# Four groups of projections in a two-layer decoder trunk: two matmuls per weight tile in place of three

## The chip, the cores and the metric

One core of one Trainium2 chip runs the whole kernel in one launch. The metric is the device time of one execution in microseconds; the kernel before was run three times, and its median is what a changed kernel is compared with.

## The reference, cut to what matters

The input `x` is 256 tokens by 1024 channels. Each of two layers does three things in turn: a SwiGLU feed-forward net, a mixing block, a second feed-forward net. Everything is float32.

```python
h = h + 0.5 * swiglu(rms_norm(h, ln_ffn1[l]), ffn1_w13[l], ffn1_w2[l])
u = rms_norm(h, ln_mix[l])
z, xbc, dt_raw, cq, ckv, kr, gates = split_cols(u @ w_in[l], IN_SPLIT_SIZES)
y_ssd = ssd_branch(z, xbc, dt_raw, ...)        # conv, Mamba-2 scan, norm, w_ssd_out
y_mla = mla_branch(cq, ckv, kr, ...)           # low-rank queries and keys, attention, w_mla_out
g = jax.nn.sigmoid(gates)
merged = g[..., :D_MODEL] * y_ssd + g[..., D_MODEL:] * y_mla
h = h + merged @ w_o[l]
```

The change touches the columns of `u @ w_in` that give the latents `cq` (512 columns) and `ckv` (256), the rotary key `kr` with `dt_raw` (96 columns, padded to 128), the first 128 channels of both gates, and the product of the attention output with `w_mla_out`.

## The kernel before

Activations lie transposed, 128 channels on the partitions by 256 tokens, and every product is a sum over blocks of 128 input channels. To keep float32 accuracy each operand is split in two parts: a high part in the type fp32r (what a copy to that type leaves) and a low part, the rest. For a weight block the high part `wh` is a cast by ScalarE (L152) and the low part `wl` a subtraction by VectorE (L153); both are at most 128 by 1024 and come from a ring of four buffers filled by a 512 KB load on the SP queue (`ahead`, L144). For an activation, `operand` (L198) makes the two parts and lays them side by side in one tile `[128, blocks, 512]`: 256 columns high, 256 columns low.

A product keeps three of the four partial products. `mm` (L164) makes three matmuls of 256 columns per weight tile, all into the same 256 columns of PSUM: `wh` by the high part (L169), `wh` by the low part (L170), `wl` by the high part (L171). `mm2` (L173) makes two: `wh` by all 512 columns (L178), which leaves two halves side by side in one PSUM bank, and `wl` by the high part into the first half (L179). The two halves must then be added: `halves` (L181) copies the second to SBUF on ScalarE (L182) and adds the first on VectorE (L183). Before the change, `mm2` serves the feed-forward nets, the gates 1 to 7 and the output product of the scan (`wso`); `mm` serves the rest.

The mixing block `mix` (L418) goes in this order. It sums the squares of the residual per token on TensorE and takes an inverse square root in some eight small VectorE instructions (`row_factor`, L245; the last of them, L224, is kept as `self.last`). Inside `issue_after(self.last)` (L437), a block whose VectorE instructions may not be queued ahead of that last one, it runs the products of the un-normalised input `X0` (an `oT` tile) with the blocks `dk` (rotary key and dt), `gate` (two blocks into the two halves of one PSUM bank) and the first of six latents. `latent(i)` (L428) runs one product, then makes an operand of the result for blocks 16 to 21 of tile `A` (ScalarE L204, VectorE L205) and squares it into a sum (`square_into`, L227). ScalarE copies of the gate (L446) and of `dk` (L448) follow. Then the normalised input `X` is built (L449 to L457), between the latents 1 to 3, then latents 4 and 5, then a long chain of small VectorE instructions for `dt` (L501 to L530) that ends in a copy `acum`, its transpose, and a store and reload through DRAM on the POOL queue (`rows`, L537; `row`, L623), on which the decay factors of the scan wait on ScalarE (L648). The loop (L546) begins with the first queries (L695, which read blocks 16 to 19 of `A`), keys and values (`keyval`, L719, blocks 20 and 21) and convolutions (L589).

At the end of `mix`, for each of eight output blocks (L553), two `wso` weight blocks go through `mm2` and `halves`, one `wmo` block goes through `mm`, and VectorE multiplies its PSUM by the second gate (L565), adds the scan's part (L566) and makes an operand of `M`, which the eight `wo` products (L570) read.

There are eight PSUM banks: four for the tag `g` of all these products, two for `s`, two for `h`. The order of the instructions on each engine is not the order of the code: a planner simulates the program with its own costs and issues, on each engine, what is ready, earlier code first. Each engine then runs its queue strictly in that order.

Of the kernel before, what the change touches and what calls it, by code (L numbers as in the profile page):

```python
# [16 lines left out]
ALU = mybir.AluOpType  # L17

P = 128
L = 2  # L20
T = 256
D = 1024
KD = D // P
# [37 lines left out]
class Build:  # L61
# [356 lines left out]
    def mix(self, l, X0, Xn, gain, gain_next):  # L418
        nc, v = self.nc, self.vec[l]
        tt, ts, stt = nc.vector.tensor_tensor, nc.vector.tensor_scalar, nc.vector.scalar_tensor_tensor  # L420
# [4 lines left out]
        A = self.new_A()  # L425
        acc2 = [self.tmp("Rb", [P, T], bufs=1), self.tmp("accs", [P, 2, T], bufs=1)[:, 0, :]]

        def latent(i):  # L428
            q = int(i > 3)
            ps = self.gps()[:, :T]  # L430
            self.mm(ps, self.w("lat"), KD, X0, 0, True, True)
            o = V_QL + i
            self.operand(A, 16 + i, ps, v[:, o:o + 1])
            self.square_into(acc2[q], ps, i in (0, 4))


        with self.tc.issue_after(self.last):  # L437
            ps = self.gps()[:, :T]
            self.mm(ps, self.w("dk"), KD, X0, 0, True, True)
            pg = self.gps()  # L440
            for g in range(2):
                self.mm(pg[:, g * T:(g + 1) * T], self.w("gate"), KD, X0, 0, g == 0, g == 1)
            latent(0)
        Rb = self.bcast(Rt, None)
        gg = self.tmp("g0", [P, 2, T], bufs=1)
        nc.scalar.copy(gg, pg.rearrange("p (g t) -> p g t", g=2))  # L446
        dk = self.tmp("ta", [P, T])
        nc.scalar.copy(dk, ps)  # L448
        X = self.new_X()  # L449
        for n in range(0, KD, 2):  # L450
            u = self.tmp("t2", [P, 2, T])
            for i in range(2):
                stt(out=u[:, i, :], in0=self.hT[:, n + i, :], scalar=gain[:, n + i:n + i + 1], in1=Rb,
                    op0=ALU.mult, op1=ALU.mult)
            hi, lo = X[:, n:n + 2, :T], X[:, n:n + 2, T:]
            nc.scalar.copy(hi, u)
            tt(out=lo, in0=u, in1=hi.bitcast(F32), op=ALU.subtract)  # L457
            if n < 6:
                latent(1 + n // 2)
# [6 lines left out]
        for c in range(2):  # L466
            act(out=tm[:, c, :], in_=pt[:, c * P:(c + 1) * P], func=AF.Copy, scale=Rt[:, c:c + 1])
        latent(4)
        latent(5)

# [3 lines left out]
        ps = self.sps()  # L474
# [36 lines left out]
        q = self.tmp("dtq", [P, 2, 32], bufs=1)  # L511
# [29 lines left out]
        oT = self.new_oT()  # L541
# [11 lines left out]
        for n in range(KD):  # L553
            gg = S["gate", n]
            stt(out=gg[:, 0, :], in0=gg[:, 0, :], scalar=1.0, in1=Rsb, op0=ALU.add, op1=ALU.mult)
            ts(out=gg[:, 1, :], in0=gg[:, 1, :], scalar1=0.5, scalar2=0.5, op0=ALU.mult, op1=ALU.add)
            ps = self.gps()
            self.mm2(ps, self.w("wso"), 8, A, 0, True, False)
            self.mm2(ps, self.w("wso"), 8, A, 8, False, True)
            m = self.tmp("ta", [P, T])  # L560
            self.halves(m, ps)
            tt(out=gg[:, 0, :], in0=gg[:, 0, :], in1=m, op=ALU.mult)
            ps = self.gps()[:, :T]
            self.mm(ps, self.w("wmo"), 8, oT, 0, True, True)
            tt(out=m, in0=gg[:, 1, :], in1=ps, op=ALU.mult)  # L565
            tt(out=m, in0=m, in1=gg[:, 0, :], op=ALU.add)  # L566
            self.operand(M, n, m)
        for n in range(KD):
            ps = self.gps()[:, :T]
# [340 lines left out]
```

## Time and profile before

| | us |
|---|---|
| median of three runs | 1467.56 |
| lowest and highest | 1466.51, 1470.18 |
| the profiled execution | 1469.72 |
| its span, first to last instruction | 1467.8 |
| TensorE busy (matmuls) | 1451.8 |
| VectorE busy | 1114.6 |
| ScalarE busy | 911.8 |

The profiled execution took 2.2 us longer than the median and 1.9 us longer than its own span. A matmul's busy time in the profile overlaps that of the next one, since they are pipelined; how fast a stream of them goes is read from the distance of their starts. "PE" is TensorE, "PEld" its weight loads, "DVE" VectorE, "ACT" ScalarE, "POOL" GpSimd. "L178" is line 178 of the kernel. Tile names are those of the program: `g` a PSUM bank of the products, `wh` and `wl` the weight parts, `oT`, `X` and `A` operand tiles.

### The profile page before, as it was taken

What the parts mean: (1) busy time and instruction counts of PE and PEld (TensorE: products, weight loads), DVE (VectorE), ACT (ScalarE), POOL (GpSimd) and SP (SyncE); (2) the same over time, 40 slices, a digit from 0 to 9 for tenths busy, and PEclk for the clock granted to TensorE, in tenths of its full rate; (3) what the DMA queues carried; (4) which work ended last, traced back from release to release, by engine and by line L of the source; (5) the groups of instructions that cost most, each with busy time, mean ns of one, the idle gap of its engine ahead of it and who ended that gap; (6) DMA issues with size and microseconds to landing.
All of it is one profiled execution on the core that took longest, in us unless ns stands there. A gap on an engine that the chain in (4) does not pass through costs nothing.

```text
span 1467.8 us, 25011 instructions
## 1 busy us (share of the span) xinstructions
PE 1451.8 (99%) x9418; PEld 1304.8 (89%) x9418; DVE 1114.6 (76%) x2080; ACT 911.8 (62%) x1738; POOL 18.5 (1%) x38
## 2 busy tenths in 40 slices
PE   7999999999999999999999999999999999999999
PEld 6888899899888999888888888997998889988888
DVE  7877679888877677777678776888888576688764
ACT  6555556988775456555455554678888654565542
POOL 0000000000000000000000000000000000000000
PEclk9999999999999999999999999999999999999999
DMA  7556655555444555556655566565554445555563
GB/s 254 184 186 178 192 176 182 183 160 157 152 144 158 188 179 188 191 189 183 193 191 191 188 180 195 178 192 155 166 169 139 154 165 190 175 190 193 187 197 109
DMA packets 75977, 261.43 MB, mean 178 GB/s; under 512 B 8880, under 2 KB 11184, under 8 KB 75856
## 3 DMA queue, kind: packets, MB, share of 16 engines
q1 hardware_dynamic: 73232, 251.37, 53.3%
q0 software_dynamic: 2624, 8.46, 1.9%
q8 instruction: 74, 1.21, 0.3%
q14 instruction: 47, 0.39, 0.1%
HBM read 258.68 MB, written 1.11 MB: 177 GB/s over the span
## 4 chain that ended last, share of the span: by engine, by line
PE 97%; DVE 1%; ACT 1%; issue 0%; DMA 0%; SPq 0%; DVEq 0%; ACTq 0%
PE g L178 40%; PE g L179 21%; PE g L169 9%; PE g L170 9%; PE g L171 9%; PE g L695 2%; PE s L658 2%; PE g L719 1%; PE h L780 1%; PE h L779 1%; PE h L761 0%; PE s L635 0%; PE h L803 0%; DVE wl L153 0%; DVE cy L594 0%; PE h L799 0%
## 5 line engine op out<-in xcount | busy, mean ns | idle before, releaser
L152 ACT CAST wh<-st 128x1024 fp32r<-128x1024 f32 (+2 forms) x488 | 500.6, 1027 | 483.5 <-PE g L178 314.7
L153 DVE TENSOR_TENSOR wl<-st,wh 128x1024 fp32r<-128x1024 f32 (+2 forms) x488 | 581.0, 1192 | 258.6 <-ACT wh L152 254.7
L178 PE MATMUL g<-X,wh 128*128 128x512 f32 x928 | 330.8, 399 | 8.0 <-DVE X L205 7.5
L178 PE MATMUL g<-A,wh 128*128 128x512 f32 x938 | 327.6, 395 | 0.0
L179 PE MATMUL g<-X,wl 128*128 128x256 f32 x928 | 262.6, 283 | 0.0
L179 PE MATMUL g<-A,wl 128*128 128x256 f32 x938 | 260.8, 279 | 0.0
L178 PE MATMUL g<-oT,wh 128*128 128x512 f32 x704 | 244.5, 392 | 0.0
L169 PE MATMUL g<-X,wh 128*128 128x256 f32 x768 | 219.6, 287 | 1.2 <-DVE cy L594 1.2
L178 PEld LDWEIGHTS g<-X,wh 128*128 128x128 f32 x928 | 175.8, 189 | 49.3 <-DVE X L205 8.3
L170 PE MATMUL g<-X,wh 128*128 128x256 f32 x768 | 218.7, 285 | 0.0
L171 PE MATMUL g<-X,wl 128*128 128x256 f32 x768 | 218.4, 285 | 0.0
L178 PEld LDWEIGHTS g<-A,wh 128*128 128x128 f32 x938 | 175.7, 188 | 40.1
L179 PE MATMUL g<-oT,wl 128*128 128x256 f32 x704 | 196.9, 280 | 0.0
L179 PEld LDWEIGHTS g<-X,wl 128*128 128x128 f32 x928 | 177.1, 191 | 0.4 <-issue 0.2
L179 PEld LDWEIGHTS g<-A,wl 128*128 128x128 f32 x938 | 176.6, 188 | 0.4
L178 PEld LDWEIGHTS g<-oT,wh 128*128 128x128 f32 x704 | 131.6, 187 | 28.6
L169 PEld LDWEIGHTS g<-X,wh 128*128 128x128 f32 x768 | 146.7, 191 | 3.2 <-issue 1.6
L170 PEld LDWEIGHTS g<-X,wh 128*128 128x128 f32 x768 | 146.9, 191 | 0.7 <-issue 0.5
L171 PEld LDWEIGHTS g<-X,wl 128*128 128x128 f32 x768 | 146.9, 191 | 0.3 <-issue 0.3
L179 PEld LDWEIGHTS g<-oT,wl 128*128 128x128 f32 x704 | 133.0, 189 | 0.2
L170 PE MATMUL g<-oT,wh 128*128 128x256 f32 x272 | 76.8, 283 | 0.0
L171 PE MATMUL g<-oT,wl 128*128 128x256 f32 x272 | 76.6, 284 | 0.0
(286 smaller groups left out, 1831.0 us busy)
## 6 DMA issues: line engine op xcount, KB each, us to landing
st<-in_w_dram SPq DMA_DIRECT2D x238, 512.0 KB, 4.3
st<-in_win_dram SPq DMA_DIRECT2D x124, 512.0 KB, 4.0
st<-in_wso_dram SPq DMA_DIRECT2D x32, 512.0 KB, 4.1
st<-in_w_dram SPq DMA_DIRECT2D x32, 384.0 KB, 3.2
row<-rows POOLq DMA_DIRECT2D x32, 256.0 KB, 3.9
st<-in_wmo_dram SPq DMA_DIRECT2D x16, 512.0 KB, 4.2
st<-in_wo_dram SPq DMA_DIRECT2D x16, 512.0 KB, 3.5
st<-in_wuq_dram SPq DMA_DIRECT2D x16, 384.0 KB, 3.3
```

The source lines that it names most:

```text
L152: self.nc.scalar.copy(wh, st)
L153: self.nc.vector.tensor_tensor(out=wl, in0=st, in1=wh.bitcast(F32), op=ALU.subtract)
L169: mm(out, lhsT=wh[:, k, :], rhs=xh, start=start and k == 0, stop=False)
L170: mm(out, lhsT=wh[:, k, :], rhs=xl, start=False, stop=False)
L171: mm(out, lhsT=wl[:, k, :], rhs=xh, start=False, stop=stop and k == nk - 1)
L178: mm(out, lhsT=wh[:, k, :], rhs=X[:, x0 + k, :], start=start and k == 0, stop=False)
L179: mm(out[:, :T], lhsT=wl[:, k, :], rhs=X[:, x0 + k, :T], start=False, stop=stop and k == nk - 1)
L658: nc.tensor.matmul(py[64 * i:64 * i + 64, q * T + c * P:(q + 1) * T], lhsT=xdt[:, c, f:f + 64], rhs=r[:, i, o:o + n], start=q == 0 and c = ...
L695: nc.tensor.matmul(pc[c], lhsT=aa, rhs=ww, start=k == 0 and i == 0, stop=k == 3 and i == 2)
L719: nc.tensor.matmul(pc[c], lhsT=aa, rhs=ww[:, k, :], start=k == 0 and i == 0, stop=k == 1 and i == 2)
L779: mm(o, lhsT=qkT[:, 0, cs], rhs=qkT[:, 1, ks], start=c == 0, stop=False)
L780: mm(o, lhsT=peT[:, 0, cs], rhs=peT[:, 1, ks], start=False, stop=False)
```

## The change

The three uses below go from `mm` to `mm2` and `halves`. The latent now goes through an SBUF tile of the tag `cy` before its operand and its square; the `dk` result and both gate results go through `halves` inside the block behind `self.last`, where one ScalarE copy each stood after it; the two gate blocks take a PSUM bank each where they shared one. In the output loop the attention product is added up into `m`, and the gate multiplies `m` where it multiplied PSUM.

```diff
         def latent(i):
             q = int(i > 3)
-            ps = self.gps()[:, :T]
-            self.mm(ps, self.w("lat"), KD, X0, 0, True, True)
+            ps = self.gps()
+            self.mm2(ps, self.w("lat"), KD, X0, 0, True, True)
+            lat = self.tmp("cy", [P, 2, T])[:, 0, :]
+            self.halves(lat, ps)
             o = V_QL + i
-            self.operand(A, 16 + i, ps, v[:, o:o + 1])
-            self.square_into(acc2[q], ps, i in (0, 4))
+            self.operand(A, 16 + i, lat, v[:, o:o + 1])
+            self.square_into(acc2[q], lat, i in (0, 4))
 
 
         with self.tc.issue_after(self.last):
-            ps = self.gps()[:, :T]
-            self.mm(ps, self.w("dk"), KD, X0, 0, True, True)
-            pg = self.gps()
+            ps = self.gps()
+            self.mm2(ps, self.w("dk"), KD, X0, 0, True, True)
+            dk = self.tmp("ta", [P, T])
+            self.halves(dk, ps)
+            gg = self.tmp("g0", [P, 2, T], bufs=1)
             for g in range(2):
-                self.mm(pg[:, g * T:(g + 1) * T], self.w("gate"), KD, X0, 0, g == 0, g == 1)
+                ps = self.gps()
+                self.mm2(ps, self.w("gate"), KD, X0, 0, True, True)
+                self.halves(gg[:, g, :], ps)
             latent(0)
         Rb = self.bcast(Rt, None)
-        gg = self.tmp("g0", [P, 2, T], bufs=1)
-        nc.scalar.copy(gg, pg.rearrange("p (g t) -> p g t", g=2))
-        dk = self.tmp("ta", [P, T])
-        nc.scalar.copy(dk, ps)
         X = self.new_X()
...
             tt(out=gg[:, 0, :], in0=gg[:, 0, :], in1=m, op=ALU.mult)
-            ps = self.gps()[:, :T]
-            self.mm(ps, self.w("wmo"), 8, oT, 0, True, True)
-            tt(out=m, in0=gg[:, 1, :], in1=ps, op=ALU.mult)
+            ps = self.gps()
+            self.mm2(ps, self.w("wmo"), 8, oT, 0, True, True)
+            self.halves(m, ps)
+            tt(out=m, in0=gg[:, 1, :], in1=m, op=ALU.mult)
             tt(out=m, in0=m, in1=gg[:, 0, :], op=ALU.add)
             self.operand(M, n, m)
```

## Rows read from the trace of the kernel before

**Rows 1.** The page, busy time (us), share of the span and instructions of each engine.

```profile
PE 1451.8 (99%) x9418; PEld 1304.8 (89%) x9418; DVE 1114.6 (76%) x2080; ACT 911.8 (62%) x1738; POOL 18.5 (1%) x38
```

**Rows 2.** The page, the chain that ended last, shares of the span by engine.

```profile
PE 97%; DVE 1%; ACT 1%; issue 0%; DMA 0%; SPq 0%; DVEq 0%; ACTq 0%
```

**Rows 3.** Busy us (instructions) of PE, PEld, DVE, ACT, POOL by stretch; PEclk, DMA.

```profile
206.00:228.00 22.00, 22.00 (x180) 22.00 (x179) 21.96 (x48) 16.12 (x33) 0.00 (x0) 1.00 0.59 188
228.00:258.00 30.00, 30.00 (x238) 29.40 (x237) 26.82 (x81) 19.20 (x46) 1.71 (x3) 1.00 0.57 183
258.00:288.00 30.00, 27.80 (x193) 23.99 (x193) 26.68 (x57) 30.00 (x73) 3.22 (x6) 0.96 0.62 201
...
470.00:560.00 90.00, 90.00 (x636) 84.25 (x636) 62.29 (x102) 42.84 (x63) 0.00 (x0) 1.00 0.55 181
```

**Rows 4.** Timeline of PE where it waits, in brackets the idle us and what ended it.

```profile
285.73 0.76 PE L719 MATMUL g<-wh,A 128*128 128x512 f32 x1 [2.19 <-DVE sm L794]
...
286.72 1.05 PE L719 MATMUL g<-wh,A 128*128 128x512 f32 x2
287.57 0.63 PE L719 MATMUL g<-wl,A 128*128 128x512 f32 x1
...
1010.01 0.47 PE L719 MATMUL g<-wh,A 128*128 128x512 f32 x1 [1.13 <-DVE cy L594]
...
1013.23 0.39 PE L169 MATMUL g<-X,wh 128*128 128x256 f32 x1 [0.94 <-DVE cy L594]
```

**Rows 5.** Groups of instructions by line and shape: xcount | busy us, mean ns | idle.

```profile
L169 PE MATMUL g<-oT,wh 128*128 128x256 f32 x272 | 76.4, 283 | 0.0
...
L183 DVE TENSOR_TENSOR t<-t,g 128x256 f32<-128x256 f32 x180 | 74.0, 413 | 0.0
L182 ACT COPY t<-g 128x256 f32<-128x256 f32 x180 | 64.6, 361 | 0.5 <-PE g L179 0.5
```

**Rows 6.** Timeline of PE in the output loop: start us, us, instruction, count.

```profile
478.79 0.28 PE L169 MATMUL g<-oT,wh 128*128 128x256 f32 x1
...
481.67 0.40 PE L178 MATMUL g<-A,wh 128*128 128x512 f32 x1
...
487.31 0.28 PE L169 MATMUL g<-oT,wh 128*128 128x256 f32 x1
```

**Rows 7.** Timeline of PE in the second feed-forward net.

```profile
599.83 0.39 PE L178 MATMUL g<-oT,wh 128*128 128x512 f32 x1
...
602.60 0.39 PE L178 MATMUL g<-oT,wh 128*128 128x512 f32 x1
```

**Rows 8.** Timeline of DVE from the mixing block's start, layer 0, then layer 1.

```profile
206.11 3.49 DVE L153 TENSOR_TENSOR wl<-st,wh 128x1024 fp32r<-128x1024 f32 x3
...
226.66 0.42 DVE L234 TENSOR_TENSOR Rb<-Rb,sq 128x256 f32<-128x256 f32 x1
227.00 1.22 DVE L153 TENSOR_TENSOR wl<-st,wh 128x1024 fp32r<-128x1024 f32 x1
...
228.27 0.48 DVE L205 SCALAR_TENSOR_TENSOR A<-g,vec,A 128x256 fp32r<-128x256 f32 x1
...
953.15 0.47 DVE L205 SCALAR_TENSOR_TENSOR A<-g,vec,A 128x256 fp32r<-128x256 f32 x1
```

**Rows 9.** Timelines of DVE and PE, last block of M and its first reader.

```profile
536.07 0.42 DVE L202 TENSOR_TENSOR X<-ta,X 128x256 fp32r<-128x256 f32 x1 [0.47 <-ACT X L201]
...
538.59 0.52 PE L169 MATMUL g<-X,wh 128*128 128x256 f32 x3
```

**Rows 10.** Timeline of PE, first keys and values, layer 0, then layer 1.

```profile
229.84 0.48 PE L719 MATMUL g<-wh,A 128*128 128x512 f32 x1
...
231.09 0.62 PE L719 MATMUL g<-wh,A 128*128 128x512 f32 x2
...
956.28 0.62 PE L719 MATMUL g<-wh,A 128*128 128x512 f32 x2
```

**Rows 11.** Timeline of ACT, first decay factors of layer 0.

```profile
257.76 1.49 ACT L648 ACTIVATE dec<-row,acum 128x256 f32<-128x256 f32 x4 [3.58 <-DMA row<-rows]
```

## The prediction

> **What bounds the kernel.** I read the busy times first, then the chain that ended last, then starts on TensorE's timeline, and last the stretches around the change. TensorE is busy 99% of the span [rows 1], and the chain of waits runs 97% through it [rows 2], so a shorter product pays one for one wherever nothing else holds TensorE up. Both shares say nothing of a single stage, though. Three stretches count here. In the output loop VectorE is busy 62.3 of 90 us and ScalarE 42.8 [rows 3], so there is room. At the start of mix, from 206 to 228 us, VectorE is busy 21.96 of 22 us [rows 3]: there it is full, though TensorE does not yet wait. From 258 to 288 us ScalarE is busy all 30 us and VectorE 26.7, and TensorE loses time: L719 waits 2.19 us in layer 0, and in layer 1 there are waits of 1.13 and 0.94 us [rows 3, 4]. The change adds work to VectorE exactly where it is full.
>
> **What TensorE saves.** The edits touch 8 blocks of 128 channels for dk, 16 for the gates, 48 for six latents and 64 for eight wmo products, 136 in a layer and 272 in all, the count of L169 on `oT` tiles [rows 5]. Each goes from three matmuls of 256 columns to one of 512 and one of 256. The columns are 768 both ways, so only the loss per instruction can shrink. What it is comes from distances of starts:
> - three by 256: a wmo product starts at 478.79 and the next wso product at 481.67, 2.88 us for 8 blocks, 0.360 us a block [rows 6];
> - two: the 16 blocks of wso from 481.67 to 487.31 take 5.64 us, 0.3525 a block [rows 6]; in the second feed-forward net, whose moving operand is the same tag `oT`, eight pairs take 602.60 - 599.83 = 2.77 us, 0.346 a block [rows 7].
>
> So a block gains 0.0075 us (slow pairs) to 0.0135 us (fast pairs). For the 144 blocks at the start of mix I take the fast pair, which has their operand and follows the same kind of stage: 1.9 us. For the 128 blocks of wmo I take the slow pair, measured next to them in the same loop: 1.0 us. Sum 2.9 us; ends 272 x 0.0075 = 2.0 and 272 x 0.0135 = 3.7 us. That is 0.2% of the time.
>
> A page speaks against this. The Trainium skill, page "TensorE: Matmul & The Clock Gate", section "Back-to-back issue gap", puts a matmul of N columns at N/2.4 + 2.5 ns, so that a fused pair saves one floor of 2.5 ns a block; by it 272 blocks would give 0.7 us in place of 2.9, an estimate. By that rule three matmuls of 256 columns would take 3 x 109 = 328 ns, where the trace has 360 [rows 6], so it agrees in the sign and not in the size.
>
> **What VectorE and ScalarE get.** Each product gains one 256-column addition on VectorE and mostly one copy on ScalarE. A lone addition takes 413 ns and a copy 361 ns [rows 5], but a queue that is full goes by distances of starts: an addition of this shape starts at 226.66 and the next instruction at 227.00, 0.34 us [rows 8]. A layer gets nine additions at the start of mix (dk, two gates, six latents) and eight in the output loop.
> - Output loop: 8 x 0.34 = 2.7 us on VectorE and at most 8 x 0.36 = 2.9 us on ScalarE, beside 90 us of TensorE with 27.7 and 47.2 us to spare [rows 3]: nothing. Without that cover it would be 5.4 us on VectorE in both layers. At its end the chain of the last block grows by a copy and an addition, 0.77 us: its low part is written by 536.07 + 0.42 = 536.49 and the first matmul that needs it starts at 538.59 [rows 9], so 2.1 us of cover, less 0.5 us by which TensorE comes earlier. Nothing, unless a weight split of 1.22 us also slips in between; then 0.4 us.
> - Start of mix: 9 x 0.34 = 3.1 us in a full queue. The copies are covered, since ScalarE has 5.9 of 22 us free [rows 3], and the gate and dk copies replace copies. All nine additions are behind `self.last` or later; the splits just behind it run back to back from 206.11 [rows 8], so the idle time ahead of it cannot be used.
> - Banks: before, dk, both gates and the first latent need three of the four `g` banks, after, all four, and the second latent waits until dk's addition, queued right behind the first split, at about 206.11 + 1.16 + 0.34 = 207.6 us. The second latent starts some 2.9 us after the first at the earliest, past 209 us. Nothing; if the planner put all the splits ahead of it, TensorE would wait about 1 us a layer.
> - The operand and the square now read SBUF in place of PSUM. An addition with one input in PSUM takes 413 ns [rows 5], one wholly in SBUF 0.42 us [rows 8]; at 0.01 us for 12 VectorE instructions this is 0.1 us in the full queue, and I take nothing.
>
> **What is late next.** Queued behind the additions on VectorE are the weight splits, the operands and the small chain of dt. The first product to feel it is keyval. The low part of block 21 is done at 228.27 + 0.48 = 228.75 us and read by the matmul at 231.09, 2.34 us of margin; in layer 1 at 953.62 against 956.28, 2.66 us [rows 8, 10]. The backlog of 3.1 us and TensorE's own 0.97 us (72 blocks x 0.0135) turn this into waits of 1.7 and 1.4 us, 3.1 us together, if the planner leaves keyval where it is. If it sees the lateness and moves convolutions ahead, it costs nothing. Both are open; I take half, 1.5 us.
>
> **The sum.** The profiled execution took 1469.72 us: minus 2.9, plus 1.5, gives 1468.3. It stands 2.16 us above the median of the runs, 1467.56, and the same difference on that gives **1466.2 us**. The ends of this case: all lateness and the slow pairs, -2.0 + 3.1 = +1.1, or 1468.7; none and the fast pairs, -3.7, or 1463.9. A measurement of this kernel can tell about 0.3% from no change, 4.4 us, so 1463.2 and 1472.0 are the bounds.
>
> **The rivals.**
> - Slower: the backlog passes on. The decay factors on ScalarE begin when `row` has landed, after 3.58 us idle [rows 11], and the load hangs on the dt chain, which sits in the same VectorE queue. If the 3.2 us that VectorE has free from 228 to 258 us [rows 3] are waits for weight buffers that TensorE frees, they don't take up the backlog; `row` comes up to 3.1 us later in each layer, ScalarE's full stretch starts as much later, and the wait at 285.73 grows. TensorE's gain ahead of it is then worth nothing; 2 x 3.1 - 1.0 (wmo) = +5.2. A longer wait in layer 1 can also bring what layer 0 shows: the granted clock falls (mean 0.96 in that stretch, the level of 1.2 GHz in it) and L719 then runs at (287.57 - 286.72)/2 = 0.43 us a matmul in place of (231.09 - 229.84)/5 = 0.25 [rows 3, 4, 10], 6 x 0.18 = 1.1 us. Together +6.3, 1473.9 us. It decides from the point where `row` is more than about 2.7 us late per layer, for 2 x 2.7 - 1.0 = 4.4. For it: a full VectorE and a full ScalarE. Against: by 228 us TensorE already binds, and a later VectorE then eats its own idle time.
> - Faster by more than 0.3%: the planner's new order happens to spread the work of 258 to 288 us, and the three waits (2.19 + 1.13 + 0.94 = 4.3) and the slow matmuls (1.1) go: -2.9 - 5.4 = -8.3, 1459.3 us. For it: these waits are a matter of order, since layer 0 and layer 1 run the same code and differ. Against: nothing in the edit takes work off either engine in that stretch.
> - The pairs save nothing in their new place: in the output loop the 512-column matmul already takes some 0.3525 - 0.120 = 0.23 us, nearly two of 0.120 [rows 6]. With 0 saved and 0 to 3.1 us of lateness: 1467.6 to 1470.7. Against: both stages measured have pairs faster than 0.360 us [rows 6, 7]. By the section of the Trainium skill named above this would be nearly the case, with 0.7 us saved, an estimate.
>
> **How the numbers follow.** The forecast case gets 0.42, no gain 0.13, the slower one 0.25 and the faster one 0.20. Of the slower case 0.02 and of the faster one 0.03 stay within 0.3%, so: same 0.42 + 0.13 + 0.02 + 0.03 = 0.60, faster 0.17, slower 0.23. The range runs from the forecast's lower end 1463.9 on into the faster case and from 1470.7 into the slower one, to 1461.0 and 1473.0, leaving out about half of each, 2 in 10. The likeliest case alone is 1463.9 to 1468.7.
>
> **What would show it.** Right: L178 on `oT` up by 272 and the lines of `mm` on it gone; starts 0.346 to 0.3525 us apart for a pair in wmo and latents; VectorE still full from 206 to about 231 us; L719 first waiting on VectorE in the order of 1.5 us, or convolutions ahead of it; VectorE's busy time up by 34 x 0.41 = 14 us and ScalarE's by about 10. The slower rival shows `row` landing over 2.7 us later in its layer and waits at the second L719 that have grown. The faster one shows those waits gone. I am wrong in the sum if pairs in wmo start 0.36 us apart, and wrong in the place if TensorE waits in the output loop.

## The result, and the profile after the change

The change made the kernel slower: median 1480.86 us of four runs (1479.45 to 1484.15) against 1467.71 us of the kernel before beside it, a ratio of 1.0093 [1.0079, 1.0107], or 13.1 us. I had forecast 1466.2 us, a range up to 1473.0 and a chance of 0.23 for slower. The execution profiled after the change took 1479.45 us, its span is 1477.6 us; before, the span was 1467.8 us, so the two traces differ by 9.8 us. In all the runs told of below, one execution (of the kernel with the work alone in six buffers) took 4540.4 us, and its ratio leaves it out. New lines shift the numbers: after, the first queries are L698 (before L695), keyval is L722 (L719), the scan's product L661 (L658), the decay factors L651 (L648).

First the page's busy times of the kernel after:

```profile
PE 1452.7 (98%) x9146; PEld 1291.0 (87%) x9146; DVE 1127.6 (76%) x2114; ACT 917.5 (62%) x1768; POOL 18.5 (1%) x38
```

Against [rows 1], VectorE has 13.0 us more (I had 14) and ScalarE 5.7 us more (I had about 10). TensorE is as busy as before, 1452.7 against 1451.8 us, though it has 272 matmuls fewer, and idle for longer. To see where, I cut the kernel at a line that both have: L241 begins a sum of squares on TensorE, once at the end of each stage. From TensorE's timeline of the kernel after (start, length in us):

```profile
203.11 0.50 PE L241 MATMUL s<-ones,acc 128*128 128x1 f32 x4
...
567.24 0.50 PE L241 MATMUL s<-ones,acc 128*128 128x1 f32 x4
...
935.74 0.50 PE L241 MATMUL s<-ones,acc 128*128 128x1 f32 x4
...
1295.20 0.50 PE L241 MATMUL s<-ones,acc 128*128 128x1 f32 x4
```

and of the kernel before:

```profile
203.92 0.51 PE L241 MATMUL s<-ones,acc 128*128 128x1 f32 x4
...
561.49 0.50 PE L241 MATMUL s<-ones,acc 128*128 128x1 f32 x4
...
929.12 0.50 PE L241 MATMUL s<-ones,acc 128*128 128x1 f32 x4
...
1285.44 0.50 PE L241 MATMUL s<-ones,acc 128*128 128x1 f32 x4
```

The mixing block of layer 0 grew from 357.57 to 364.13 us (+6.56), that of layer 1 from 356.32 to 359.46 (+3.14). The mark is not quite the start of the block: TensorE runs products of `dk` and the gates ahead of it, and after the change it runs more of them there. The first of these in layer 1 starts, after the change, at

```profile
929.61 0.40 PE L178 MATMUL g<-oT,wh 128*128 128x512 f32 x1
```

and in the kernel before at

```profile
923.85 0.28 PE L169 MATMUL g<-oT,wh 128*128 128x256 f32 x1
```

That is 6.13 and 5.27 us ahead of the mark; in layer 0 it starts at 196.87 and 198.65, 6.24 and 5.27 us ahead. Counted from these starts the blocks grew by 7.53 and 4.00 us, the nets between them take 362.37 us against 362.36, and the end changed by +0.04; only the first feed-forward net differs otherwise, by -1.78 (the last section tells why it can). The whole loss is in the two mixing blocks. Now the stretches of the two blocks, and those of [rows 3], after (columns as there: length, then busy time of PE, PEld, DVE, ACT, POOL, granted clock, DMA share, GB/s):

```profile
203.11:567.24 364.13, 355.68 (x2433) 318.83 (x2432) 289.04 (x606) 253.48 (x537) 9.22 (x17) 1.00 0.51 164
935.74:1295.20 359.46, 354.56 (x2434) 319.55 (x2432) 287.05 (x597) 252.96 (x536) 9.11 (x17) 1.00 0.51 166
...
206.00:228.00 22.00, 19.74 (x111) 16.49 (x109) 22.00 (x49) 15.14 (x32) 0.00 (x0) 1.00 0.63 196
470.00:560.00 90.00, 90.00 (x579) 81.98 (x578) 67.48 (x120) 45.93 (x72) 0.00 (x0) 1.00 0.56 184
...
385.00:395.00 10.00, 7.39 (x29) 5.20 (x29) 9.77 (x26) 6.41 (x22) 0.00 (x0) 0.83 0.48 159
```

The same blocks in the kernel before:

```profile
203.92:561.49 357.57, 355.38 (x2561) 326.75 (x2560) 281.96 (x589) 250.75 (x522) 9.22 (x17) 1.00 0.52 167
929.12:1285.44 356.32, 353.97 (x2560) 325.33 (x2559) 281.16 (x580) 249.80 (x521) 9.11 (x17) 1.00 0.52 168
```

The time in which TensorE is not busy is the difference of the first two numbers: after 8.45 and 4.90 us, before 2.19 and 2.35. That is 8.8 us of the 11.5; in the rest TensorE shows as busy, though the pairs should have shortened that. What TensorE waited for in the two blocks after (total us, times, longest; layer 0, then layer 1):

```profile
PE h L806 <- ACT pT L804: 3.6, 2, 2.2
PE g L698 <- DVE cy L183: 1.7, 1, 1.7
PE g L722 <- DVE cy L597: 1.4, 1, 1.4
...
PE g L698 <- DVE cy L183: 1.6, 1, 1.6
PE g L169 <- ACT vv L748: 0.9, 1, 0.9
PE s L638 <- DVE rqy L224: 0.8, 1, 0.8
```

Before, layer 0 had one such wait worth a row, the 2.2 us of L719 that I had listed [rows 4]. Now there are two kinds. One stands where the change was made: the first queries wait for a latent's addition (`cy`, L183). The others stand further on, in attention and convolutions: in layer 0 at 287.56 and 290.33 us, near where L719 waited before, and at 388.41, 160 us behind the queries. On TensorE's timeline of the kernel after:

```profile
227.96 0.41 PE L698 MATMUL g<-wh,A 128*128 128x384 f32 x1 [1.75 <-DVE cy L183]
...
232.17 0.47 PE L722 MATMUL g<-wh,A 128*128 128x512 f32 x1 [0.29 <-DVE cy L183]
...
388.41 0.70 PE L806 MATMUL h<-pT,vv 128*128 128x256 f32 x2 [2.20 <-ACT pT L804]
...
390.26 1.05 PE L722 MATMUL g<-wh,A 128*128 128x512 f32 x2
391.12 0.63 PE L722 MATMUL g<-wl,A 128*128 128x512 f32 x1
```

After the 2.20 us of waiting, two matmuls of L722 take (391.12 - 390.26)/2 = 0.43 us each, against 0.25 in [rows 10]; the granted clock of the 10 us around is 0.83 on average, so part of it ran at the level of 1.2 GHz; by that mean up to 10 x 0.17 = 1.7 us of work was lost, an estimate.

**Why the queries wait.** The wait of 1.75 us ends with the addition of the fourth latent, on VectorE's timeline

```profile
227.39 0.42 DVE L183 TENSOR_TENSOR cy<-cy,g 128x256 f32<-128x256 f32 x1
```

and so done at 227.81 us. A query does not read that tile, though. It writes a PSUM bank `g`; the four banks are handed out in turn, and by the code the query's second bank is the one that held the fourth latent's product, which the addition is the last to read. The matmul starts at 227.96, 0.15 us behind it. So I read it as a wait for a bank, not for an operand; no run tests that.

The addition itself comes late, and so does all that follows it. The latents pass through two buffers of the tag `cy` (a tag has two buffers unless the code says otherwise). ScalarE's timeline after shows the copies of the first five:

```profile
211.29 0.36 ACT L182 COPY cy<-g 128x256 f32<-128x256 f32 x1
...
214.53 0.37 ACT L182 COPY cy<-g 128x256 f32<-128x256 f32 x1
...
219.50 0.35 ACT L182 COPY cy<-g 128x256 f32<-128x256 f32 x1
...
224.78 0.36 ACT L182 COPY cy<-g 128x256 f32<-128x256 f32 x1
...
228.67 0.38 ACT L182 COPY cy<-g 128x256 f32<-128x256 f32 x1
```

and VectorE's timeline the low parts, the last to read their buffers, of the first three latents and of the sixth:

```profile
217.89 0.48 DVE L205 SCALAR_TENSOR_TENSOR A<-cy,vec,A 128x256 fp32r<-128x256 f32 x1
...
222.45 0.49 DVE L205 SCALAR_TENSOR_TENSOR A<-cy,vec,A 128x256 fp32r<-128x256 f32 x1
...
228.19 0.40 DVE L205 SCALAR_TENSOR_TENSOR A<-cy,vec,A 128x256 fp32r<-128x256 f32 x1
...
234.33 0.48 DVE L205 SCALAR_TENSOR_TENSOR A<-cy,vec,A 128x256 fp32r<-128x256 f32 x1
```

A latent holds its buffer from the copy to the end of the low part; the first three hold it for 218.37 - 211.29 = 7.1, 222.94 - 214.53 = 8.4 and 228.59 - 219.50 = 9.1 us, the last three for 3.8 to 4.7. The third copy comes after the first low part, the fifth (228.67) 0.08 us after the third low part (228.59), with the end of the fourth latent's square between them on ScalarE. Two buffers held for some 8 us pass one latent in 4 us, where TensorE makes one in 8 pairs, 2.8 us; the six copies, 211.29 to 230.24, are 3.8 us apart. That is the reading of the trace; the runs below test it.

### The profile page after: what moved, and what is told of

Read it like the earlier page. It is cut to its first block, busy times and chain, and to the rows that moved or that the text cites. A ratio compares the mean times of both kernels' runs of the same rounds, so it can differ in the third digit from the quotient of the medians.

```text
span 1477.6 us, 24546 instructions
## 1 busy us (share of the span) xinstructions
PE 1452.7 (98%) x9146; PEld 1291.0 (87%) x9146; DVE 1127.6 (76%) x2114; ACT 917.5 (62%) x1768; POOL 18.5 (1%) x38
## 4 chain that ended last, share of the span: by engine, by line
PE 51%; issue 42%; DVE 3%; ACT 2%; DMA 1%; SPq 0%; POOL 0%; ACTq 0%; DVEq 0%; POOLq 0%
PE g L178 22%; PE g L179 11%; PE g L169 4%; PE g L170 4%; PE g L171 4%; PE g L698 1%; DVE wl L153 1%; PE s L661 1%; PE g L722 1%; PE h L783 1%; ACT dec L651 1%; PE h L782 1%; DMA row<-rows 1%; ACT wh L152 1%; DMA rows<-pp 1%
## 5 line engine op out<-in xcount | busy, mean ns | idle before, releaser
L178 PE MATMUL g<-oT,wh 128*128 128x512 f32 x976 | 340.9, 393 | 0.0
L178 PE MATMUL g<-X,wh 128*128 128x512 f32 x928 | 327.7, 397 | 8.0 <-DVE X L205 7.5
L178 PE MATMUL g<-A,wh 128*128 128x512 f32 x938 | 327.2, 394 | 0.0
L169 PE MATMUL g<-X,wh 128*128 128x256 f32 x768 | 220.1, 288 | 1.2 <-ACT vv L748 0.9
L171 PE MATMUL g<-X,wl 128*128 128x256 f32 x768 | 218.4, 285 | 0.0
L178 PEld LDWEIGHTS g<-oT,wh 128*128 128x128 f32 x976 | 182.7, 187 | 39.9
L178 PEld LDWEIGHTS g<-X,wh 128*128 128x128 f32 x928 | 175.3, 189 | 47.8 <-DVE X L205 8.3
L178 PEld LDWEIGHTS g<-A,wh 128*128 128x128 f32 x938 | 175.7, 188 | 39.8
L179 PEld LDWEIGHTS g<-oT,wl 128*128 128x128 f32 x976 | 184.9, 189 | 0.5 <-DVE wl L153 0.3
L169 PEld LDWEIGHTS g<-X,wh 128*128 128x128 f32 x768 | 146.8, 192 | 3.3 <-ACT vv L748 1.2
L171 PEld LDWEIGHTS g<-X,wl 128*128 128x128 f32 x768 | 146.8, 191 | 0.2 <-issue 0.2
L183 DVE TENSOR_TENSOR t<-t,g 128x256 f32<-128x256 f32 x180 | 74.3, 415 | 0.0
L597 DVE SCALAR_TENSOR_TENSOR cy<-g,vec,cy 128x255 f32<-128x255 f32 (+1 forms) x144 | 68.2, 478 | 0.2
```

The lines of the kernel that those rows point to most:

```text
L169: mm(out, lhsT=wh[:, k, :], rhs=xh, start=start and k == 0, stop=False)
L171: mm(out, lhsT=wl[:, k, :], rhs=xh, start=False, stop=stop and k == nk - 1)
L178: mm(out, lhsT=wh[:, k, :], rhs=X[:, x0 + k, :], start=start and k == 0, stop=False)
L179: mm(out[:, :T], lhsT=wl[:, k, :], rhs=X[:, x0 + k, :T], start=False, stop=stop and k == nk - 1)
L183: self.nc.vector.tensor_tensor(out=out, in0=out, in1=ps[:, :T], op=ALU.add)
L597: nc.vector.scalar_tensor_tensor(out=y[:, i, k:], in0=ps[:, :T - k], scalar=v[:, w0 + 3 - k:w0 + 4 - k], in1=y[:, i, k:], op0=ALU.mult, op ...
```

## The experiments

Two questions in turn: which part of the change costs the time (the latents, `dk` and the gates behind `self.last`, or the output loop), and what it is in that part (the pairs, the added work on VectorE and ScalarE, or the two buffers). Each kernel starts from the kernel before. Totals are medians, with the ratio to the kernel before that ran beside it and, in brackets, its 95% interval.

**Parts of the change.** Only the output loop:

```diff
-            ps = self.gps()[:, :T]
-            self.mm(ps, self.w("wmo"), 8, oT, 0, True, True)
-            tt(out=m, in0=gg[:, 1, :], in1=ps, op=ALU.mult)
+            ps = self.gps()
+            self.mm2(ps, self.w("wmo"), 8, oT, 0, True, True)
+            self.halves(m, ps)
+            tt(out=m, in0=gg[:, 1, :], in1=m, op=ALU.mult)
```

> Only the attention output (wmo) goes to pairs, the start of mix stays as before. Three theories for the 13 us by which the whole change is slower. A, the latent chain: each latent now passes a copy, an addition, a cast and a subtraction on two engines through two cy buffers, the queries wait for it, and the loss is made at the start of mix. B, the planner: any edit gives the loop a new order with new waits. C, the output loop itself got slower. A expects 2 to 4 us less than before (1464 to 1466), since TensorE binds in the output loop; B expects layer 0 up to the output loop unchanged and a shift of either sign, up to 5 us, in layer 1; C expects at least 5 us more than before.

Measured: 1466.5 us, 0.999 [0.998, 0.9999], 1.4 us less than the 1467.9 of before. This part is a small gain, only just clear of the noise. In its profiled execution both mixing blocks, from their first product, are 1.3 us shorter than before (361.54 and 360.25).

The start of mix alone is the change without that last hunk of its diff:

> The latents, dk and the gates in pairs, wmo as before. A expects the whole loss and the gain of wmo missing: 15 to 17 us over before, with the wait of the first queries for the addition of a latent (1.6 to 1.8 us in each layer) still there. B expects a loss too, but not tied to that wait. C expects no more than 3 us over before.

Measured: 1487.39 us, 1.0132 [1.0115, 1.0149]. The edits at the start of mix alone lose more than the whole change does, 19.5 us where A had 15 to 17. The first queries wait for an addition here too, 1.9 us in layer 0 and 1.6 in layer 1.

Only the latents:

```diff
         def latent(i):
             q = int(i > 3)
-            ps = self.gps()[:, :T]
-            self.mm(ps, self.w("lat"), KD, X0, 0, True, True)
+            ps = self.gps()
+            self.mm2(ps, self.w("lat"), KD, X0, 0, True, True)
+            lat = self.tmp("cy", [P, 2, T])[:, 0, :]
+            self.halves(lat, ps)
...
-            self.operand(A, 16 + i, ps, v[:, o:o + 1])
-            self.square_into(acc2[q], ps, i in (0, 4))
+            self.operand(A, 16 + i, lat, v[:, o:o + 1])
+            self.square_into(acc2[q], lat, i in (0, 4))
```

> Only the six latents in pairs, with their copy and addition. A expects 6 to 15 us over before, with the first queries waiting for the addition of a latent. B expects any shift between -5 and +10 us. C expects no change beyond 3 us.

Measured: 1479.83 us, 1.0082 [1.0067, 1.0097], about 12 us. Of all parts this one carries the loss. But the sign that A named is missing: in neither layer do the first queries wait for the addition of a latent, only 0.4 us for the high part of one (A, L204) in layer 0. So that wait, although it stands first in the trace of the change, is not what the 12 us hang on.

Only `dk` and the gates (the hunk inside `issue_after`), and of these only `dk`:

```diff
         with self.tc.issue_after(self.last):
-            ps = self.gps()[:, :T]
-            self.mm(ps, self.w("dk"), KD, X0, 0, True, True)
+            ps = self.gps()
+            self.mm2(ps, self.w("dk"), KD, X0, 0, True, True)
+            dk = self.tmp("ta", [P, T])
+            self.halves(dk, ps)
...
-        dk = self.tmp("ta", [P, T])
-        nc.scalar.copy(dk, ps)
```

> Only dk and the two gate blocks in pairs, latents as before. A expects 0 to 2 us over or under before: three additions of 0.34 us in a full VectorE queue against 48 blocks times 0.013 = 0.6 us saved on TensorE. B expects a shift of up to 8 us with no wait at the first queries. C expects no change beyond 1 us.

> Only dk in pairs, the gates as before in one shared bank. dkgate_only took 2.7 us more than before. If the gates' second bank or their two additions cost it, dk_only is within 1 us of before; if dk's addition, queued behind the inverse square root ahead of its transposes and the dt chain, costs it, 2 to 3 us over before.

Measured: 1470.6 us, 1.0017 [1.0008, 1.0027], and 1470.52 us, 1.0014 [1.0005, 1.0024]. In total `dk` alone costs as much as `dk` and the gates, 2.7 us, a little more than the 2 us that A allowed for both. ScalarE's timeline of the kernel with `dk` alone shows the decay factors of layer 0:

```profile
258.76 2.88 ACT L648 ACTIVATE dec<-row,acum 128x256 f32<-128x256 f32 x8 [3.81 <-DMA row<-rows]
```

Its mix begins at 201.78 us (L241), so they start 56.98 us in, against 257.76 - 203.92 = 53.84 before [rows 11]: 3.1 us later, though only one addition was put in. Its first scan product (L658) starts 61.74 us after the start of mix, against 59.64 before, and waits 0.76 us for the decay factors. This is the path that I had named for the slower rival; in its profiled execution the mixing block of layer 0, from its first product, is 2.1 us longer than before and that of layer 1 as long. With the gates added, the decay factors and the first scan product are as late (56.44 and 62.99 us into mix), but the blocks grow by 0.5 and 1.1 us. So the two kernels do not lose their time in the same place, and a late scan alone does not set the loss. In the whole change this path isn't the one that decides: there `dec` starts at 253.74, 50.63 us into mix, earlier than before.

The parts don't add up cleanly: latents, `dk` with gates, and output loop give +12, +2.7 and -1.4, together +13, but the first two in one kernel give +19.5. The planner orders each kernel anew; which of its choices costs the difference was not separated.

**Pairs, work, or buffers?** Four kernels change the latents alone. One gives each pair of latents its own tag, six buffers in all (the line is shown against the kernel with only the latents in pairs):

```diff
-            lat = self.tmp("cy", [P, 2, T])[:, 0, :]
+            lat = self.tmp(("cy", "BC", "xs")[i // 2], [P, 2, T], bufs=XSB if i > 3 else None)[:, 0, :]
```

> The latents alone in pairs, as in lat_only, but their sums go to six buffers (two each of the tags cy, BC and xs) in place of two of cy, so that no latent waits for the one two ahead of it to be released. If the two cy buffers are what holds the latents apart, most of the 12 us of lat_only is gone: at most 4 us over before, and the operand of the sixth latent less than 3 us later than before's 228.75 us in layer 0. If the two extra steps through full queues are the cause, it stays within 3 us of lat_only (1477 to 1483).

Measured: 1467.11 us, 0.9991 [0.9982, 1.0001]. The loss of 12 us is gone, with every matmul, copy and addition in place.

One has the pairs and adds nothing:

```diff
-            ps = self.gps()[:, :T]
-            self.mm(ps, self.w("lat"), KD, X0, 0, True, True)
+            ps = self.gps()
+            self.mm2(ps, self.w("lat"), KD, X0, 0, True, True)
+            ps = ps[:, :T]
```

> The latents alone in pairs, but nothing is added: operand and square read the first half in PSUM, as before, and the product of the high weights with the low part of the activations is left out. If the additions and their chain are the cause, this is as fast as before or up to 2.6 us faster (96 blocks x 0.0135 x 2 halves at most), 1465 to 1468, and the queries don't wait. If the pairs themselves or a new order of the planner are the cause, 5 us or more over before.

Measured: 1468.78 us, 1.0001 [0.9991, 1.001], 0.8 us above what was expected but level with before. The pairs are not the cost.

One keeps three matmuls and does a copy and an instruction of the addition's shape, through the two `cy` buffers; operand and square then read `lat`:

```diff
             self.mm(ps, self.w("lat"), KD, X0, 0, True, True)
+            lat = self.tmp("cy", [P, 2, T])[:, 0, :]
+            nc.scalar.copy(lat, ps)
+            tt(out=lat, in0=lat, in1=ps, op=ALU.max)
...
```

> The latents keep their three matmuls, but the result passes a copy on ScalarE and a maximum with itself on VectorE into a cy buffer, the same two instructions of the same size as in the paired form, and operand and square read that. If the chain of extra steps is the cause, it is as slow as lat_only or 1 us slower: 1477 to 1484, with the queries waiting for the VectorE step on cy. If the pairs on TensorE matter, it stays within 3 us of before.

Measured: 1479.98 us, 1.0076 [1.0061, 1.0091], the full loss without a pair, and again no wait of the queries for the VectorE step. The same work through the six buffers:

> As lat_work, three matmuls for each latent and then a copy and a maximum, but into six buffers. Buffers theory: the 11.8 us of lat_work go, 1467 to 1471, with the work on VectorE and ScalarE unchanged. If the work is what costs, 1477 to 1482 as lat_work.

Measured: 1468.13 us, 1.0 [0.9991, 1.001]. So with buffers enough the work on VectorE and ScalarE costs nothing that can be measured either.

**Depth, or sharing `cy` with the convolutions?** The convolutions use `cy` too. Two buffers of another tag, and four buffers, `cy` among them (again against the kernel with only the latents in pairs):

```diff
-            lat = self.tmp("cy", [P, 2, T])[:, 0, :]
+            lat = self.tmp("xs", [P, 2, T], bufs=XSB)[:, 0, :]
```

```diff
-            lat = self.tmp("cy", [P, 2, T])[:, 0, :]
+            lat = self.tmp(("cy", "BC")[i % 2], [P, 2, T])[:, 0, :]
```

> The latents in pairs as in lat_only, with two buffers, but of the tag xs, which the first convolution's sums don't use. If depth is the cause, it is as slow as lat_only, 1476 to 1484. If sharing cy with the convolutions is, it is near lat_ring, 1465 to 1470.

> The latents in pairs as in lat_only, in four buffers, two of cy and two of BC taken in turn; the last two latents hold one of each. If depth is the cause: a latent holds its buffer for about 7 to 8 us in the whole change's trace, two buffers pass one latent in 4 us against TensorE's 2.8, four pass one in 2 us and are enough, so 1465 to 1470. If sharing cy is the cause, the fifth latent still holds a cy buffer when the convolutions begin, and it stays 4 us or more over before.

Measured: 1479.19 us, 1.008 [1.0065, 1.0096], and 1467.05 us, 0.9992 [0.9983, 1.0002]. Depth decides; whose buffers they are does not. Three buffers were not tried.

All these kernels set side by side, each in its own profiled execution. "Operand" is the end of the sixth latent's low part (L205) and "scan" the start of the first scan product, both in layer 0 and counted from L241 at the start of mix; the last columns are the lengths of the two mixing blocks from L241 to L241. All rows but that of the change have the same work ahead of the mark (5.27 to 5.29 us); the change has 0.97 and 0.86 us more there, which its lengths lack.

| kernel | buffers | operand | scan | mix 0 | mix 1 |
|---|---|---|---|---|---|
| before | none | 24.83 | 59.64 | 357.57 | 356.32 |
| the change | 2 | 31.70 | 64.47 | 364.13 | 359.46 |
| latents only | 2 | 30.62 | 67.33 | 366.02 | 360.37 |
| latents, two of `xs` | 2 | 30.61 | 66.03 | 363.84 | 360.28 |
| work only | 2 | 30.97 | 67.66 | 366.37 | 360.36 |
| latents, four | 4 | 28.45 | 59.43 | 356.27 | 355.17 |
| latents, six | 6 | 28.45 | 59.39 | 356.79 | 356.93 |
| work, six | 6 | 28.46 | 60.00 | 357.16 | 355.29 |

Two things are to be seen. The additions make the last operand 28.45 - 24.83 = 3.6 us later even with buffers enough, and that costs nothing: the first scan product starts 0.2 us earlier than before with the pairs, 0.4 later with the work alone. With six buffers ScalarE's first and last copy are 13.66 us apart, 2.7 us a latent in place of 3.8, near the pace of TensorE:

```profile
211.54 0.37 ACT L182 COPY cy<-g 128x256 f32<-128x256 f32 x1
...
225.20 0.36 ACT L182 COPY xs<-g 128x256 f32<-128x256 f32 x1
```

The missing buffers make it another 2.2 to 3.3 us later, and then the scan starts 4.8 to 8.0 us later. The trace of the kernel with only the latents shows where the time goes, on TensorE's timeline:

```profile
232.77 0.33 PE L763 MATMUL h<-cb,qn 128*128 128x128 f32 x1 [1.51 <-ACT qn L706]
...
234.28 0.63 PE L721 MATMUL g<-wl,A 128*128 128x512 f32 x1
234.71 0.41 PE L169 MATMUL g<-X,wh 128*128 128x256 f32 x1
234.93 0.42 PE L170 MATMUL g<-X,wh 128*128 128x256 f32 x1
...
238.24 0.63 PE L721 MATMUL g<-wh,A 128*128 128x512 f32 x2
...
395.13 0.58 PE L169 MATMUL g<-X,wh 128*128 128x256 f32 x1 [2.53 <-DVE cy L596]
```

and in its stretches:

```profile
204.53:570.55 366.02, 360.18 (x2512) 327.01 (x2511) 285.62 (x595) 251.82 (x528) 9.22 (x17) 0.99 0.51 163
...
228.00:240.00 12.00, 10.41 (x54) 9.20 (x53) 9.54 (x34) 6.60 (x22) 0.00 (x0) 0.86 0.50 167
385.00:400.00 15.00, 12.47 (x65) 10.75 (x64) 12.78 (x39) 10.64 (x32) 0.00 (x0) 0.80 0.43 142
```

Keyval (L721), one block of twelve matmuls before [rows 10], is torn in two: four of its matmuls, then convolutions (L169 to L171) until 238.24, then the rest. Each of the two stretches holds a wait and, behind it, a lowered clock: by its mean up to 12 x 0.14 = 1.7 and 15 x 0.20 = 3.0 us of work lost, an estimate, at the level of 1.2 GHz, where 256 columns go 234.93 - 234.71 = 0.22 us apart in place of 0.12 [rows 6]. With six buffers keyval is split as well, but among the matmuls of the queries and not by convolutions, and the block of layer 0 shows 356.79 - 354.30 = 2.5 us without work in place of 5.8:

```profile
202.80:559.59 356.79, 354.30 (x2513) 322.54 (x2511) 283.30 (x595) 251.38 (x528) 9.25 (x17) 1.00 0.52 167
```

The block with two buffers is 9.2 us longer: 3.3 us of it are idle time, 5.9 are time in which TensorE shows as busy, and the lowered clock is up to 4.7 of these. The three kernels with two buffers (pairs in `cy`, pairs in `xs`, work only) have the same waits of TensorE in layer 0 to a tenth of a us: 3.6 for convolutions, 1.5 for the matmul behind the first queries (L763 or L764), 0.4 at the first queries, 0.2 for keyval. The three with four or six have others: 1.2 for keyval, the rest at most 0.7. As far as these waits show, the number of buffers picks between two orders of the same work, and the loss goes with the order.

**The change mended.** The whole change with six buffers for the latents, and the same with `dk` and gates left as before:

> The whole change, with six buffers for the latents in place of two. Buffers theory: the 12 us of the latents go, and 1466 to 1470 is left (-1.4 wmo, -1.1 latents, +2.7 dk and gates). If the loss of the whole change comes from VectorE's nine additions at the start of mix, which are all still there, at least 8 us over before.

> The two parts that did no harm: wmo in pairs, and the latents in pairs with six buffers; dk and gates as before. The buffers theory adds what was measured for each alone, -1.4 (wmo_only) and -1.1 (lat_ring): 1464 to 1467, the fastest of all. If the parts don't add, because the planner's order differs again, anything from 1462 to 1475.

Measured: 1469.18 us, 1.0007 [0.9998, 1.0017], and **1463.67 us, 0.997 [0.9957, 0.9983]**. The first is only level with the kernel before: in its profiled execution the mixing blocks, from their first product, take 362.40 and 361.12 us against 362.84 and 361.59. Its first scan product starts 61.92 us into mix, 2.3 us later than before, near the 61.74 of `dk` alone, but its decay factors are not late, and I did not find out why. The second is faster than both kernels, a little more than the sum of the parts had it; its mixing blocks take 354.69 and 354.15 us. It and the kernel before were profiled once more, for the distances of starts told of below:

> wmo_ring, unchanged. If the level belongs to the kernel as built, the first feed-forward net again shows 0.349 and the output loop 0.347 us a pair. If it belongs to the single execution, some stage changes level.

> The kernel before, unchanged. If the level of the pairs belongs to the kernel as built, the first feed-forward net and the output loop again show 0.355 and 0.353 us a pair. If it belongs to the single execution, some stage changes level.

Measured: 1464.85 and 1468.34 us; mixing blocks 354.65 and 354.08 us, and 356.73 and 356.35.

## Why the prediction was wrong

**The step that failed** is the term for the start of mix, "9 x 0.34 = 3.1 us in a full queue". I sized the lateness by VectorE's throughput alone. Even for the work it was too small: with six buffers and all nine additions (the whole change mended) the operand is 29.30 - 24.83 = 4.5 us late, with the six of the latents alone 3.6 us. And I had read that the latent "now goes through an SBUF tile of the tag `cy`" and never asked how many such tiles there are, or how long each is held. With two, the operand is 31.70 - 24.83 = 6.9 us late, twice my figure. The price of a buffer held by two engines in turn is missing from the sum: with the latents alone, four more buffers take away all of the 12 us.

**"If it sees the lateness and moves convolutions ahead, it costs nothing"** held in its outcome for 3.6 us (four and six buffers), where the planner moved keyval in among the queries, and failed for 5.8 to 6.9 us (two). There convolutions did come ahead; yet the new order brought its own waits, 160 us later too, and half-speed stretches behind them. I had bounded this case by 3.1 us for both layers; it cost about 12. I can't say how much of that is the order and how much the waits, because the planner's order can't be held while the buffers change; that stays open.

**The first to feel it** in the whole change was not keyval, as I had said, but the first queries: 1.75 us in layer 0 and 1.6 in layer 1, until a latent's addition had ended; keyval waited 0.29 us. If that is a wait for a PSUM bank, as read above, then the banks, which I had put at "nothing" after looking at the second latent only, were wrong as well. With the latents alone the queries don't wait so, and the loss is there all the same.

**The slower rival** had the sign, and the wrong mechanism for the whole change. Its `row` does land 3.1 us later where `dk` alone is changed, and that kernel is 2.7 us slower; in the whole change `row` is 3.2 us earlier. Its lowered clock after a longer wait did appear, again in layer 0.

**The faster rival** came in small, in the second mended kernel: the three waits of 2.19, 1.13 and 0.94 us are gone from its traces, and TensorE's idle time in the two blocks is 3.2 us in its second execution against 5.2 in that of the kernel before.

**What was right.** The pairs are faster than three matmuls. Three starts of the output loop after the change:

```profile
494.19 0.39 PE L178 MATMUL g<-oT,wh 128*128 128x512 f32 x1
...
496.96 0.39 PE L178 MATMUL g<-A,wh 128*128 128x512 f32 x1
...
502.51 0.39 PE L178 MATMUL g<-oT,wh 128*128 128x512 f32 x1
```

A wmo product takes 2.77 us for 8 blocks, 0.346 a block, against 0.360 before [rows 6]. I had taken the slow pair, 0.3525, by its neighbour; but the neighbour changed too, and wso now takes 5.55/16 = 0.347. At the start of mix it is the other way round: I had taken the fast pair, and after the change the latents' pairs start 0.353 us apart (with the latents alone 0.347). Both guesses were wrong, and 128 x 0.0133 + 144 x 0.0067 = 2.7 us comes near my 2.9 by luck. The output loop's cover held: VectorE 67.48 and ScalarE 45.93 of 90 us, TensorE 90.00. The loop alone gave -1.4 us where I had -1.0. By the floor of 2.5 ns in the Trainium skill, page "TensorE: Matmul & The Clock Gate", section "Back-to-back issue gap", which the section gives for a single matmul by itself and not for a sustained stream, 128 blocks would have saved an estimated 128 x 2.5 ns = 0.3 us; the totals don't tell these apart, the distances of starts in this stream (0.014 us a block) speak against it. L178 on `oT` rose by 272 to 976, as the change says.

## What to carry to other kernels

Where an edit sends a result through a rotating buffer on its way between two engines, divide the time that one result holds the buffer (here 7 to 9 us, read from the copy's start to its last reader's end) by the time in which results are made (2.8 us). Here that gives about three; two cost 12 us and four nothing, with the same work on the engines. A planner that simulates the program can answer a late operand with another order far away, so costs of parts need not add: here a lateness of 3.6 us was free, and one of about 6 us went with a loss of 12. Compare two such kernels between marks that both have, and not by totals alone, and see whether the same work lies ahead of the mark in both. A wait that shows first in a trace need not be the one that costs: here a smaller edit kept the loss and lost the wait.

## What was not expected of the hardware

The same pairs go at one of two speeds, even through a whole stage. In the first feed-forward net, two executions of the same mended kernel differ. Eight pairs on TensorE's timeline of its first profile:

```profile
99.31 0.39 PE L178 MATMUL g<-X,wh 128*128 128x512 f32 x1
...
102.08 0.39 PE L178 MATMUL g<-X,wh 128*128 128x512 f32 x1
```

and of its second:

```profile
99.28 0.40 PE L178 MATMUL g<-X,wh 128*128 128x512 f32 x1
...
102.11 0.40 PE L178 MATMUL g<-X,wh 128*128 128x512 f32 x1
```

2.77 against 2.83 us. Mix of layer 0 starts at 200.27 us in the one and at 204.31 in the other, and the difference stays at 3.9 to 4.0 us to the start of the last stage. In the output loop the level belonged to the kernel instead: both profiled executions of the kernel before have 0.353 us a pair in both layers, both of the mended one 0.347. With the output loop alone changed it is 0.353 in layer 0 and 0.347 in layer 1. What sets the level was not found. It means that a part of the mended kernel's gain of some 4 us is this level and not the pairs: an estimated 256 x 0.006 = 1.5 us for the wso pairs, which no edit touches. Another part is the waits that are gone; the shares were not separated. The first feed-forward net, ahead of every edit, ends between 195.0 and 201.1 us in the profiled executions of all these kernels; so differences of 1 us between medians here should not be explained, nor those of some us between single executions.
